# Program order on four engines at the output projections' boundaries of a two-block network, on one Trainium2 core

## The chip, the cores and the metric

The kernel runs on one core of one Trainium2 chip. The metric is the device time of a whole execution in microseconds (us). Its engines each work through a queue of their own: PE (TensorE) multiplies, ACT (ScalarE) and DVE (VectorE) work on elements, POOL (GpSimd) does small work and issues a part of the DMAs, SP (SyncE) issues most DMAs. Semaphores alone tie the queues together, so an instruction that waits holds whatever stands behind it on its own engine.

## The reference

Two blocks over x of 512 tokens by 1024 features, batch 1, all in fp32. The first block mixes by two kinds of attention, attends to a memory of 256 tokens and ends with a swiglu layer. The second block has two layers with a condition c and positions: an mLSTM mixer and a latent attention (MLA), each followed by a squared-relu layer. What matters here is the frame around each part:

```python
mix = jnp.concatenate([o_f, o_c], axis=-1) @ w_out[l]
x = x + rms_norm(mix, g_mix_post[l])
h = rms_norm(x, g_mem_pre[l])
...
x = x + g1[:, None, :] * rmsnorm(y, norm_g[l, 1])
h = modulate(rmsnorm(x, norm_g[l, 2]), sh2, sc2)
```

The shifts, scales and gates of the second block come from `cond @ ada_w[l] + ada_b[l]`, a vector times a matrix of 1024 by 6144 in each layer, and a smaller matrix `kv_ada_w`.

## The kernel before, in words

The tokens are four row tiles of 128, t = 0 to 3. x lies in SBUF as `x[t]`; before a product its normed rows are transposed, so that features lie on the partitions. Each fp32 product is three matmuls of a hi and a lo part (`prod`, lines 447 to 449). A weight block of 512 KB comes by DMA into one of four `raw` buffers (L423, SP's queue) and is split there: ACT writes the hi part (L307, or L317 with a gain), DVE subtracts it and writes the lo part (L308, L318). A block gives up its `raw` buffer when its last split is placed, which is when the next load can start. `pump` does this counting, `BUF["raw"]` is its limit, and `self.before` lists loads of x that go out ahead of a numbered weight block.

**A boundary** is where the output of one stage becomes the input of the next (`boundary`, L637). For each row tile t, `y_of(t)` multiplies (24 matmuls of 128x512 for the second half of an output projection), the squares of the result are summed on ACT (L579, `junk`), POOL makes a reciprocal root of it (`rstd`: L568, L562), DVE scales and adds it to x (L651, two halves), ACT squares the new x (L579), POOL makes the second `rstd`, and ACT writes the normed rows (L598, two halves). Then `put(t)`: eight transposes on PE (L609), in two stages of the network four scaled and shifted blocks on DVE (L616) and four on ACT (L619), then the hi part on ACT (L629, two) and the lo part on DVE (L630, two). With `fixed`, put(0) stands in the middle of product t = 2 and put(1) in the middle of product t = 3. The generator `first` is the head of the next stage: four accumulators of 24 matmuls of 128x256 for the tokens of row tiles 0 and 1 (tok0), then four for tiles 2 and 3 (tok1). So PE restarts with put(1)'s parts, and can hold out until tok1 needs put(2) and put(3).

`out_lin` (L716) calls `boundary` four times, with `fixed`: after `w_out`, after `w_mem_o`, after `a_w_out` and after `b_w_out`. I call these the first to the fourth boundary. Only the third and fourth scale and shift. `mlp` (L1344) calls it as well: after the swiglu (fixed), after the first squared-relu layer (not fixed), and for the last rows, where nothing follows.

**The order of the work** on each engine is not the order of the code. A scheduler plays the program through a simulated timeline and gives each engine its list. Work inside `hot` (`self.hot("hb")`) is lifted by a priority offset of 300. `ordered` (L692), which nothing called before, keeps the order of the code on PE, ACT, DVE and POOL for what it encloses.

Beside the main work, background steps compute the condition's rows (`row_by`, L859): pieces of `ada_w` come by POOL's DMAs (L878) into `araw`, DVE multiplies and adds them up (L873), folds the sum and splits it (L630), and then one matmul against a matrix of ones on PE (L891, the ones product) adds up over the partitions. Each `yield` ends a step; a step is taken for every 1.9 us of PE's work, and none inside a boundary.

The functions that the change touches, and those that call them:

Of the kernel before, what the change touches and what calls it, by code (L numbers as in the profile page):

```python
# [30 lines left out]
D_FF = 2816  # L31
ALL = slice(0, S)

BUF = dict(s8=14, u2=15, row=2, raw=4, w0=4, w1=4, w2=4, w3=5, w4=5, w5=5, w6=5, w7=5, ps=8, pace=1.9, pacb=1.9, man=0, lag=3, lagx=3, lagm=3, half=1, quiet=1, xp=0, fp=2, r1=1.25, r1b=3.6, r1c=2.4, r2=1.6, r2b=2.6, rx=1.4, rm=0.6, pre=10, gl=3, pl=0, hb=300, hs=0, ha=0, sp=0, spq=1.3, sq=1, b1=1, b2=1, lc=6, ar=4, mb=(6, 8, 6, 6, 6), mc=(4, 3, 4, 4, 4), st2=1, pr2=8, z1=4.5, z2=5, gt=3, rv=2, gs=1, rl=3, n1=4, ex=2, em=3, vg=1, sb=(8, 8, 6), mo=4, x1=2, g0=20, st=1, y1=0, y2=1, y3=0, ph=0, pq=0, fy=1, u1=6, s32=4, sm=60)

TWO_PI = 2.0 * np.pi

# [101 lines left out]
class Net:  # L139
    def __init__(self, tc, args, out, dbg=None, specs=None, pools=None):  # L140
        self.dry = specs is None
        self.specs = [] if self.dry else specs
        self.tc, self.a, self.out, self.dbg = tc, args, out, dbg or {}
        self.nc = Nothing() if self.dry else tc.nc
        self.cp, self.sb, self.ps, self.dr = pools
        self.uid = 0
        self.bg = None
        self.pace = 0.0
        self.quiet = self.late = False
        self.have = set()  # L150
        self.n_lo = self.n_load = self.n_take = 0
        self.n_ready = 0, 0
        self.raw_live = self.w_live = 0
        self.wcap = 0
        self.raws, self.ready = {}, {}
        self.pieces, self.credit = [], 0.0
        self.started, self.n_heads = None, 0
        self.gcols, self.before = {}, {}
# [45 lines left out]
    def pump(self):  # L204
# [4 lines left out]
        while more:  # L209
            more = False  # L210
            if self.n_load < len(self.specs):
                i = self.n_load
                kk, cc, loaders = self.specs[i][:3]
                if self.raw_live + len(loaders) <= BUF["raw"]:
                    self.raws[i] = [self.t("raw", [P, kk, cc], F32, BUF["raw"]) for _ in loaders]
                    for f in self.before.pop(i, ()):
                        f()
                    for loader, raw in zip(loaders, self.raws[i]):
                        loader(self, raw)
                    self.n_load += 1  # L220
                    self.raw_live += len(loaders)
                    more = True
            i, p = self.n_ready
            if i < self.n_load and self.w_live < self.wcap:
                kk, cc, loaders, gain = self.specs[i]
# [411 lines left out]
    def boundary(self, y_of, nxt, first, late=(1, 1, 2), fixed=True):  # L637
# [18 lines left out]
        def scaled(t):  # L656
            pend[t] = nxt(t, rs[t])

        hot = lambda: self.hot("hb")
        with nullcontext():  # L660
            for t in range(NT):
                g, n = y_of(t), 0
                while True:
# [407 lines left out]
    def mixer1(self):  # L1071
# [3 lines left out]
        get = lambda t: nc.sync.dma_start(out=self.x[t], in_=a["x"][0, tt(t), :])  # L1075
# [8 lines left out]
            nc.sync.dma_start(out=ext[:, 64:256], in_=rb)  # L1084
            nc.sync.dma_start(out=far, in_=rb[:, 191:192].rearrange("h o -> (h o)").partition_broadcast(P))

        self.before = {1: [lambda: get(1)], 3: [lambda: get(2), lambda: get(3)], 6: [biases]}
        h = HT(self, KD)
        vf = self.big([P, NT, S])
        with self.in_order():  # L1090
            self.mixer1_values(h, vf, w)
        self.cap(0)

        wg = self.weights(w, 0, KD, 1536, 8, gain="mix")
# [45 lines left out]
        vs, os, st = [vf, None], [None, None], {}  # L1140
# [37 lines left out]
        f, gs = fill(), self.gains()  # L1178
# [162 lines left out]
        return ho  # L1341


    def mlp(self, blocks, up, w_down, g, nxt, first, ready=None, caps=None, fixed=True):  # L1344

        nc, V = self.nc, self.nc.vector
        acc = [[self.u2() for _ in range(2)] for _ in range(NT)]
# [1 line left out]
        for b, nb in enumerate(blocks):  # L1349
# [26 lines left out]
            if last:  # L1376
# [6 lines left out]
                        ms += part(t, c, (yield from product(t, wgs[c])))  # L1383
                    return acc[t], ms

                self.boundary(y_of, nxt, first, fixed=fixed)
            else:
                for c in range(2):
                    wg = self.weights(w_down, k0, nb, c * S, S)
# [59 lines left out]
    def relu2(self, h, l, g, nxt, first, ready=None):  # L1449
# [23 lines left out]
                quarters.extend(self.quarters(h))  # L1473

        quarters = []
        self.mlp(BUF['mb'], up, self.a["mlp_w2_2"][l], g, nxt, first, ready, BUF['mc'], fixed=nxt is None)


    VW = 129
# [507 lines left out]
```

## Time and profile before

| | us |
|---|---|
| three runs, median | 1999.02 (1995.79 to 1999.51) |
| the profiled execution | 1995.13 |
| its span | 1993.3 |
| PE busy | 1941.7 (97% of the span) |
| DVE, ACT, POOL busy | 1276.1, 1037.3, 351.5 (64, 52, 18%) |
| granted TensorE clock, mean over the span | 0.991 |

The profiled execution lies 3.9 us under the median of the three runs. The page gives busy time by engine, the chain of work that ended last, and the waits; in the chain PE holds 90%, ACT and DVE 4% each. A row of a timeline has the start and length of an instruction (or of several alike, xN), its engine, line and tiles, and in brackets how long the engine had been idle before and what released it. Consecutive matmuls overlap in it: their starts, not their lengths, give the pace.

### The profile page before, as it was taken

To read this page: it belongs to the slowest core of one execution; us is meant where nothing else is said; L and a number is where in the kernel's file an instruction comes from. 1 tells how busy PE (TensorE), PEld (TensorE's weight loads), DVE (VectorE), ACT (ScalarE), POOL (GpSimd) and SP (SyncE) were. 2 spreads that over 40 slices of the span, in tenths; PEclk is the share of its full clock that TensorE was granted. 3 is DMA by queue.
4 is the path that set the end of the run, shared out by engine and by line. 5 is a ranking of instruction groups with operands and counts; after the bars stand their busy time and mean duration, and the time that the engine had idled before them with its cause. 6 is when DMAs were issued, how large, how long until landed. Compare 5 with 4: busy or idle time off the path is not lost.

```text
span 1993.3 us, 28466 instructions
## 1 busy us (share of the span) xinstructions
PE 1941.7 (97%) x10222; PEld 1645.7 (83%) x10222; DVE 1276.1 (64%) x2517; ACT 1037.3 (52%) x2282; POOL 351.5 (18%) x703
## 2 busy tenths in 40 slices
PE   7999999998999999999998999999999999999998
PEld 5888987878888888878877888888888879989987
DVE  5756655765766785666885557654458655656765
ACT  6767775456334343455646442433566555545443
POOL 1331111211221231212232222210020012000000
PEclk9999999999999999999999999999999999999999
DMA  6332333442655563345462446533042121233222
GB/s 202 91 80 65 117 125 112 145 138 64 190 181 164 175 212 127 103 128 154 125 192 94 126 161 222 165 112 119 29 126 69 64 85 43 75 107 116 96 82 77
DMA packets 175246, 241.95 MB, mean 121 GB/s; under 512 B 20107, under 2 KB 117536, under 8 KB 175104
## 3 DMA queue, kind: packets, MB, share of 16 engines
q1 hardware_dynamic: 150704, 170.53, 27.1%
q0 software_dynamic: 24400, 69.60, 11.4%
q8 instruction: 80, 1.31, 0.3%
q14 instruction: 62, 0.51, 0.1%
HBM read 237.88 MB, written 2.20 MB: 120 GB/s over the span
## 4 chain that ended last, share of the span: by engine, by line
PE 90%; ACT 4%; DVE 4%; issue 1%; DMA 0%; POOL 0%; SPq 0%; DVEq 0%; POOLq 0%; ACTq 0%
PE ps L447 25%; PE ps L448 24%; PE ps L449 24%; PE ps L510 6%; PE ps L1033 1%; PE ps L609 1%; PE ps L1823 1%; ACT s L317 1%; PE ps L1852 1%; PE ps L1004 1%; PE ps L1583 1%; DVE s L318 1%; PE ps L1017 1%; PE ps L1320 1%; ACT junk L579 1%
## 5 line engine op out<-in xcount | busy, mean ns | idle before, releaser
L447 PE MATMUL ps<-s,s 128*128 128x512 f32 (+3 forms) x2468 | 940.2, 383 | 28.5 <-ACT s L629 28.5
L448 PE MATMUL ps<-s,s 128*128 128x512 f32 (+3 forms) x2468 | 928.3, 377 | 0.1
L449 PE MATMUL ps<-s,s 128*128 128x512 f32 (+3 forms) x2468 | 924.4, 377 | 2.0 <-DVE s L630 2.0
L447 PEld LDWEIGHTS ps<-s,s 128*128 128x128 f32 (+1 forms) x2468 | 467.2, 190 | 114.6 <-ACT s L629 31.5
L449 PEld LDWEIGHTS ps<-s,s 128*128 128x128 f32 (+1 forms) x2468 | 466.3, 189 | 91.3 <-DVE s L630 2.5
L448 PEld LDWEIGHTS ps<-s,s 128*128 128x128 f32 (+1 forms) x2468 | 467.3, 189 | 83.7 <-DVE s L630 1.0
L307 ACT ACTIVATE s<-raw 128x512 fp32r<-128x512 f32 x329 | 186.3, 623 | 177.3 <-PE ps L449 130.7
L308 DVE TENSOR_TENSOR s<-raw,s 128x512 fp32r<-128x512 f32 x329 | 213.9, 688 | 87.8 <-ACT s L307 85.9
L873 DVE SCALAR_TENSOR_TENSOR u<-araw,cond,u 128x512 f32<-128x512 f32 x224 | 168.5, 752 | 31.9 <-DMA araw<-in_ada_w 21.9
L317 ACT ACTIVATE s<-raw,cols_all 128x256 fp32r<-128x256 f32 (+1 forms) x305 | 142.7, 544 | 59.5 <-PE ps L449 25.2
L318 DVE SCALAR_TENSOR_TENSOR s<-raw,cols_all,s 128x256 fp32r<-128x256 f32 (+1 forms) x305 | 146.2, 538 | 30.8 <-ACT s L317 30.5
L878 POOL DMA_DIRECT2D araw<-in_ada_w x192 | 104.2, 543 | 283.2 <-DVE u L873 236.2
L630 DVE TENSOR_TENSOR s<-u,s 128x512 fp32r<-128x512 f32 x118 | 80.1, 689 | 115.1 <-ACT s L629 92.6
L510 PEld LDWEIGHTS ps<-s,s 128*128 128x128 f32 x1092 | 130.2, 188 | 1.0
L568 POOL TENSOR_SCALAR sm<-sm,sm 128x1 f32<-128x1 f32 x34 | 16.5, 485 | 647.8 <-ACT junk L579 519.8
L510 PE MATMUL ps<-s,s 128*128 128x256 f32 x1092 | 130.5, 280 | 0.0
L629 ACT ACTIVATE s<-u 128x512 fp32r<-128x512 f32 x118 | 72.2, 627 | 53.6 <-PE ps L449 27.0
L630 DVE TENSOR_TENSOR s<-ps,s 128x512 fp32r<-128x512 f32 (+3 forms) x100 | 59.5, 606 | 36.9 <-ACT s L629 35.8
L1465 ACT ACTIVATE u<-ps 128x512 f32<-128x512 f32 x38 | 22.6, 596 | 114.9 <-PE ps L449 111.0
L1368 DVE TENSOR_TENSOR u<-ps,u 128x512 f32<-128x512 f32 x80 | 54.3, 687 | 39.7 <-PE ps L449 39.6
L629 ACT ACTIVATE s<-ps 128x512 fp32r<-128x512 f32 (+3 forms) x100 | 51.2, 526 | 23.5 <-PE ps L609 10.2
L318 DVE SCALAR_TENSOR_TENSOR s<-raw,cols_mix,s 128x128 fp32r<-128x128 f32 (+2 forms) x152 | 52.4, 401 | 11.0 <-ACT s L317 10.6
(261 smaller groups left out, 2011.0 us busy)
## 6 DMA issues: line engine op xcount, KB each, us to landing
raw<-in_mlp_w SPq DMA_DIRECT2D x128, 512.0 KB, 3.8
araw<-in_ada_w POOLq DMA_DIRECT2D x192, 256.0 KB, 3.4
raw<-in_w_gate_up SPq DMA_DIRECT2D x44, 512.0 KB, 4.5
raw<-in_w_in SPq DMA_DIRECT2D x24, 512.0 KB, 4.1
raw<-in_a_w_in SPq DMA_DIRECT2D x24, 512.0 KB, 4.6
raw<-in_w_down SPq DMA_DIRECT2D x22, 512.0 KB, 3.8
raw<-in_w_mem_kv SPq DMA_DIRECT2D x16, 512.0 KB, 3.5
araw<-in_kv_ada_w POOLq DMA_DIRECT2D x32, 256.0 KB, 3.6
```

What stands on the lines that cost most here:

```text
L307: A.activation(hi[:, sl, cl], src[:, sl, cl], AF.Copy)
L308: f.tensor_tensor(out=lo[:, sl, cl], in0=src[:, sl, cl], in1=hi[:, sl, cl].bitcast(F32), op=ALU.subtract)
L317: A.activation(hi[:, i, :], src[:, i, :], AF.Copy, scale=g)
L318: V.scalar_tensor_tensor(out=lo[:, i, :], in0=src[:, i, :], scalar=g, in1=hi[:, i, :].bitcast(F32), op0=ALU.mult, op1=ALU.subtract)
L447: self.nc.tensor.matmul(ps, lhsT=ah, rhs=bh, start=first and i == 0, stop=False)
L448: self.nc.tensor.matmul(ps, lhsT=ah, rhs=bl, start=False, stop=False)
L449: self.nc.tensor.matmul(ps, lhsT=al, rhs=bh, start=False, stop=last and i == n - 1)
L510: nc.tensor.matmul(ps, lhsT=l[:, k, :], rhs=m[:, k, :], start=first and k == e == 0, stop=k == 3 and e == 2, skip_group_check=True)
L629: self.nc.scalar.activation(hi, x, AF.Copy)
L630: self.nc.vector.tensor_tensor(out=lo, in0=x, in1=hi.bitcast(F32), op=ALU.subtract)
L873: V.scalar_tensor_tensor(out=acc, in0=raws.pop(j), scalar=vec[:, j:j + 1], in1=acc, op0=ALU.mult, op1=ALU.add)
L878: nc.gpsimd.dma_start(out=raws[j], in_=ws[:, j, :])
```

## The change

Three edits. (1) `out_lin`'s boundaries run inside `ordered`, so that on PE, ACT, DVE and POOL the order of the code holds, and nothing in them is lifted by `hot`; `mlp` now calls `boundary` with `fixed=False` throughout, which changes the swiglu's boundary alone: its transposes become `hot` and follow the products. (2) In the first stage three `raw` buffers may be in use rather than four, and the loads of x move: x[1] ahead of weight block 2 rather than 1, x[2] and x[3] ahead of block 4 rather than 3. SP's queue then begins x[0], gains, raw 0, raw 1, x[1], raw 2, raw 3, x[2], x[3]; before it began x[0], gains, raw 0, x[1], raw 1, raw 2, x[2], x[3], raw 3. (3) In the table `BUF`, y2 goes from 1 to 2: one more `yield` before the ones product of a background row.

```diff
@@ class Net, __init__ @@
         self.raw_live = self.w_live = 0
+        self.rcap = BUF["raw"] - 1
@@ pump @@
-                if self.raw_live + len(loaders) <= BUF["raw"]:
+                if self.raw_live + len(loaders) <= self.rcap:
@@ boundary @@
-        hot = lambda: self.hot("hb")
-        with nullcontext():
+        hot = nullcontext if fixed else lambda: self.hot("hb")
+        with self.ordered() if fixed else nullcontext():
@@ mixer1 @@
-        self.before = {1: [lambda: get(1)], 3: [lambda: get(2), lambda: get(3)], 6: [biases]}
+        self.before = {2: [lambda: get(1)], 4: [lambda: get(2), lambda: get(3)], 6: [biases]}
         h = HT(self, KD)
         vf = self.big([P, NT, S])
         with self.in_order():
             self.mixer1_values(h, vf, w)
+        self.rcap = BUF["raw"]
@@ mlp @@
-    def mlp(self, blocks, up, w_down, g, nxt, first, ready=None, caps=None, fixed=True):
+    def mlp(self, blocks, up, w_down, g, nxt, first, ready=None, caps=None):
...
-                self.boundary(y_of, nxt, first, fixed=fixed)
+                self.boundary(y_of, nxt, first, fixed=False)
@@ relu2 @@
-        self.mlp(BUF['mb'], up, self.a["mlp_w2_2"][l], g, nxt, first, ready, BUF['mc'], fixed=nxt is None)
+        self.mlp(BUF['mb'], up, self.a["mlp_w2_2"][l], g, nxt, first, ready, BUF['mc'])
```

How this moves instructions. In the rows below the line numbers of the changed kernel are one or two higher for the same code (L609 becomes L610, L629 L630, L891 L892), and tiles are named by what they are with a number: `ps` a PSUM bank, `s` a hi or lo part, `u` an SBUF row tile, `x_10` and `x_11` the row tiles t = 2 and 3.

First place: the first boundary, PE at the end of product t = 3. Before, put(1)'s transposes stood behind the product's last matmul, ahead of the next stage's first (128x256):

```order
1317 L449 MATMUL ps_3719<-s_768_3518,s_695_3173 128x512
1318 L447 MATMUL ps_3719<-s_768_3518,s_694_3172 128x512
1319 L448 MATMUL ps_3719<-s_768_3518,s_694_3172 128x512
1320 L449 MATMUL ps_3719<-s_768_3518,s_695_3173 128x512
1321 L609 MATMUL ps_3738<-ident_66,u_809_3702 128x128 x4
1322 L609 MATMUL ps_3743<-ident_66,u_810_3704 128x128 x4
1323 L447 MATMUL ps_3794<-s_802_3677,s_770_3531 128x256
1324 L447 MATMUL ps_3795<-s_802_3677,s_770_3531 128x256
1325 L448 MATMUL ps_3794<-s_803_3678,s_770_3531 128x256
1326 L449 MATMUL ps_3794<-s_802_3677,s_770_3531 128x256
```

Now they stand in the middle of the product, with twelve matmuls behind them:

```order
1307 L449 MATMUL ps_3721<-s_751_3401,s_692_3168 128x512
1308 L450 MATMUL ps_3721<-s_751_3401,s_693_3169 128x512
1309 L610 MATMUL ps_3740<-ident_66,u_809_3704 128x128 x4
1310 L610 MATMUL ps_3745<-ident_66,u_810_3706 128x128 x4
1311 L448 MATMUL ps_3721<-s_766_3505,s_694_3172 128x512
1312 L449 MATMUL ps_3721<-s_766_3505,s_694_3172 128x512
1313 L450 MATMUL ps_3721<-s_766_3505,s_695_3173 128x512
1314 L448 MATMUL ps_3721<-s_766_3505,s_694_3172 128x512
1315 L449 MATMUL ps_3721<-s_766_3505,s_694_3172 128x512
```

The same place on ACT. Before, the sixteen hi splits of four weight blocks stood ahead of put(1)'s parts (L629, last two rows):

```order
321 L579 ACTIVATE junk_3713,sm_3712<-x_10_91 128x1024
322 L317 ACTIVATE s_818_3726<-raw_3510,cols_all_1926 128x256 x4
323 L317 ACTIVATE s_819_3735<-raw_3523,cols_all_1926 128x256 x4
324 L317 ACTIVATE s_822_3758<-raw_3540,cols_all_1926 128x256 x4
325 L317 ACTIVATE s_823_3767<-raw_3557,cols_all_1926 128x256 x4
326 L579 ACTIVATE junk_3773,sm_3772<-ps_3719 128x512
327 L629 ACTIVATE s_802_3677<-ps_3738 128x4x128
328 L629 ACTIVATE s_804_3681<-ps_3743 128x4x128
```

Now two splits stand ahead of these parts (L630), and the rest of the splits behind them:

```order
318 L580 ACTIVATE junk_3715,sm_3714<-x_10_91 128x1024
319 L318 ACTIVATE s_818_3728<-raw_3510,cols_all_1926 128x256 x2
320 L630 ACTIVATE s_802_3679<-ps_3740 128x4x128
321 L630 ACTIVATE s_804_3683<-ps_3745 128x4x128
322 L318 ACTIVATE s_818_3728<-raw_3510,cols_all_1926 128x256 x2
323 L580 ACTIVATE junk_3775,sm_3774<-ps_3721 128x512
324 L599 ACTIVATE u_828_3779<-x_10_91,sm_3719 128x512
325 L599 ACTIVATE u_829_3781<-x_10_91,sm_3719 128x512
326 L580 ACTIVATE junk_3790,sm_3789<-x_11_92 128x1024
```

Second place: DVE some microseconds later, where it writes the lo parts of put(2). The casts and scalings between them (L774 ff.) belong to the tables of positions, whose numbers a DMA of POOL brings. Before, the first lo part of put(2) stood ahead of the first cast (337):

```order
333 L630 TENSOR_TENSOR s_805_3682<-ps_3743,s_804_3681 128x4x128
334 L318 SCALAR_TENSOR_TENSOR s_849_3992<-raw_3770,cols_all_1926,s_849_3992 128x256 x4
335 L318 SCALAR_TENSOR_TENSOR s_850_4009<-raw_3830,cols_all_1926,s_850_4009 128x256 x4
336 L630 TENSOR_TENSOR s_803_3678<-ps_3870,s_802_3677 128x4x128
337 L774 CAST sm_4096<-sm_4094 128x4
338 L630 TENSOR_TENSOR s_805_3682<-ps_3875,s_804_3681 128x4x128
339 L781 TENSOR_SCALAR u_861_4131<-u_860_4098,sm_4096 128x32 x4
340 L784 TENSOR_SCALAR araw_4136<-u_861_4131 128x128
341 L630 TENSOR_TENSOR s_803_3678<-ps_3918,s_802_3677 128x4x128
342 L786 CAST u_863_4138<-araw_4136 128x128
```

Now the cast (333) stands ahead of both, with splits and the tables' first steps between it and the first lo part (340):

```order
329 L652 SCALAR_TENSOR_TENSOR x_11_92<-u_776_3562,sm_3785,x_11_92 128x512
330 L652 SCALAR_TENSOR_TENSOR x_11_92<-u_827_3777,sm_3785,x_11_92 128x512
331 L319 SCALAR_TENSOR_TENSOR s_819_3737<-raw_3523,cols_all_1926,s_819_3737 128x256 x4
332 L319 SCALAR_TENSOR_TENSOR s_822_3760<-raw_3540,cols_all_1926,s_822_3760 128x256 x2
333 L775 CAST sm_4099<-sm_4097 128x4
334 L319 SCALAR_TENSOR_TENSOR s_822_3760<-raw_3540,cols_all_1926,s_822_3760 128x256
335 L782 TENSOR_SCALAR u_861_4134<-u_860_4101,sm_4099 128x32 x3
336 L319 SCALAR_TENSOR_TENSOR s_822_3760<-raw_3540,cols_all_1926,s_822_3760 128x256
337 L782 TENSOR_SCALAR u_861_4134<-u_860_4101,sm_4099 128x32
338 L785 TENSOR_SCALAR araw_4139<-u_861_4134 128x128
339 L787 CAST u_863_4141<-araw_4139 128x128
340 L631 TENSOR_TENSOR s_803_3680<-ps_3872,s_802_3679 128x4x128
```

Third place: PE behind the swiglu's boundary, where a ones product stands among the next stage's products. Before:

```order
3816 L447 MATMUL ps_8715<-s_1629_8583,s_1571_8253 128x512
3817 L448 MATMUL ps_8715<-s_1629_8583,s_1571_8253 128x512
3818 L449 MATMUL ps_8715<-s_1629_8583,s_1572_8254 128x512
3819 L891 MATMUL ps_8734<-u_1654_8711,onesr_78 128x512
3820 L447 MATMUL ps_8747<-s_1599_8388,s_1569_8249 128x512
3821 L448 MATMUL ps_8747<-s_1599_8388,s_1569_8249 128x512
```

Now the ones product of the row ahead of it in the list (128x320) comes in this stretch, 47 rows further on, and the one of before comes a hundred rows later:

```order
3863 L448 MATMUL ps_8738<-s_1613_8545,s_1562_8252 128x512
3864 L449 MATMUL ps_8738<-s_1613_8545,s_1562_8252 128x512
3865 L450 MATMUL ps_8738<-s_1613_8545,s_1563_8253 128x512
3866 L892 MATMUL ps_8768<-u_1645_8722,onesr_78 128x320
3867 L946 MATMUL ps_8799<-ident_66,u_1629_8621 128x8 x4
3868 L946 MATMUL ps_8806<-ident_66,u_1633_8629 128x8 x4
```

## Rows read from the trace of the kernel before

**Rows 1.** Page, part 1: busy us (share of the span), instructions.
```profile
PE 1941.7 (97%) x10222; PEld 1645.7 (83%) x10222; DVE 1276.1 (64%) x2517; ACT 1037.3 (52%) x2282; POOL 351.5 (18%) x703
```

**Rows 2.** Waits of PE: us in total, times, longest.
```profile
PE ps L447 <- ACT s L629: 28.5, 9, 6.1
```

**Rows 3.** Timeline of PE at the first boundary: start us, us, instruction, [idle before <-releaser].
```profile
334.21 1.04 PE L609 MATMUL ps<-ident,u 128*128 128x128 f32 x8
...
340.11 0.80 PE L447 MATMUL ps<-s,s 128*128 128x256 f32 x2 [4.86 <-ACT s L629]
...
345.59 0.28 PE L448 MATMUL ps<-s,s 128*128 128x256 f32 x1
...
347.00 0.29 PE L448 MATMUL ps<-s,s 128*128 128x256 f32 x1
```

**Rows 4.** Timeline of PE at the other three boundaries.
```profile
471.41 0.79 PE L447 MATMUL ps<-s,s 128*128 128x256 f32 x2 [5.03 <-ACT s L629]
...
475.35 0.28 PE L447 MATMUL ps<-s,s 128*128 128x256 f32 x1
...
1082.16 0.79 PE L447 MATMUL ps<-s,s 128*128 128x256 f32 x2 [6.13 <-ACT s L629]
...
1086.32 0.28 PE L447 MATMUL ps<-s,s 128*128 128x256 f32 x1
...
1640.65 0.80 PE L447 MATMUL ps<-s,s 128*128 128x256 f32 x2 [4.85 <-ACT s L629]
...
1646.84 0.28 PE L449 MATMUL ps<-s,s 128*128 128x256 f32 x1
```

**Rows 5.** Timeline of ACT at the first boundary.
```profile
332.53 6.48 ACT L317 ACTIVATE s<-raw,cols_all 128x256 fp32r<-128x256 f32 x16
...
339.48 1.06 ACT L629 ACTIVATE s<-ps 128x512 fp32r<-128x512 f32 x2
```

**Rows 6.** Timelines of POOL and DVE behind the first boundary.
```profile
346.90 0.84 POOL L201 DMA_DIRECT2D sm<-in_positions  x1
...
351.08 0.17 DVE L774 CAST sm<-sm 128x4 f32<-128x4 int32 x1 [1.55 <-DMA sm<-in_positions]
```

**Rows 7.** Timeline of ACT at the second and third boundaries.
```profile
464.22 6.08 ACT L317 ACTIVATE s<-raw,cols_all 128x256 fp32r<-128x256 f32 x15
...
1074.15 4.26 ACT L307 ACTIVATE s<-raw 128x512 fp32r<-128x512 f32 x8
...
1078.88 1.48 ACT L619 ACTIVATE u<-ps,cols,cols 128x128 f32<-128x128 f32 x4
...
1081.47 0.63 ACT L629 ACTIVATE s<-u 128x512 fp32r<-128x512 f32 x1
```

**Rows 8.** Windows: granted clock (PEclk) at a restart and around the L891 wait.
```profile
340.00:346.00 6.00, 5.84 (x27) 5.55 (x28) 5.98 (x13) 6.00 (x14) 0.56 (x1) 0.54 0.78 260
...
880.00:900.00 20.00, 17.23 (x75) 13.71 (x74) 15.01 (x21) 7.97 (x11) 4.74 (x9) 1.00 0.28 81
```

**Rows 9.** Timelines of PE and DVE at the ones product that waits.
```profile
892.62 0.47 PE L891 MATMUL ps<-u,onesr 128*128 128x512 f32 x1 [2.77 <-DVE u L630]
...
891.79 0.69 DVE L630 TENSOR_TENSOR u<-u,u 64x512 fp32r<-64x512 f32 x1
```

**Rows 10.** Timelines of PE and ACT in the first stage.
```profile
28.65 0.79 PE L447 MATMUL ps<-s,s 128*128 128x512 f32 x1 [3.30 <-ACT s L629]
...
29.66 1.91 PE L609 MATMUL ps<-ident,u 128*128 128x128 f32 x8
...
24.05 0.60 ACT L1061 ACTIVATE s<-ps 128x512 f32<-128x512 f32 x1 [2.24 <-PE ps L449]
...
29.26 5.09 ACT L317 ACTIVATE s<-raw,cols_mix 128x128 fp32r<-128x128 f32 x17
```

**Rows 11.** Timelines of POOL and DVE at the third boundary.
```profile
1079.08 2.43 POOL L568 TENSOR_SCALAR sm<-sm,sm 128x1 f32<-128x1 f32 x1 [4.40 <-ACT junk L579]
...
1077.05 4.29 DVE L308 TENSOR_TENSOR s<-raw,s 128x512 fp32r<-128x512 f32 x7
```

More of the change, by code (lines that the diff above doesn't have):

```diff
@@ L32 @@
 ALL = slice(0, S)
-BUF = dict(s8=14, u2=15, row=2, raw=4, w0=4, w1=4, w2=4, w3=5, w4=5, w5=5, w6=5, w7=5, ps=8, pace=1.9, pacb=1.9, man=0, lag=3, lagx=3, lagm=3, half=1, quiet=1, xp=0, fp=2, r1=1.25, r1b=3.6, r1c=2.4, r2=1.6, r2b=2.6, rx=1.4, rm=0.6, pre=10, gl=3, pl=0, hb=300, hs=0, ha=0, sp=0, spq=1.3, sq=1, b1=1, b2=1, lc=6, ar=4, mb=(6, 8, 6, 6, 6), mc=(4, 3, 4, 4, 4), st2=1, pr2=8, z1=4.5, z2=5, gt=3, rv=2, gs=1, rl=3, n1=4, ex=2, em=3, vg=1, sb=(8, 8, 6), mo=4, x1=2, g0=20, st=1, y1=0, y2=1, y3=0, ph=0, pq=0, fy=1, u1=6, s32=4, sm=60)
+BUF = dict(s8=14, u2=15, row=2, raw=4, w0=4, w1=4, w2=4, w3=5, w4=5, w5=5, w6=5, w7=5, ps=8, pace=1.9, pacb=1.9, man=0, lag=3, lagx=3, lagm=3, half=1, quiet=1, xp=0, fp=2, r1=1.25, r1b=3.6, r1c=2.4, r2=1.6, r2b=2.6, rx=1.4, rm=0.6, pre=10, gl=3, pl=0, hb=300, hs=0, ha=0, sp=0, spq=1.3, sq=1, b1=1, b2=1, lc=6, ar=4, mb=(6, 8, 6, 6, 6), mc=(4, 3, 4, 4, 4), st2=1, pr2=8, z1=4.5, z2=5, gt=3, rv=2, gs=1, rl=3, n1=4, ex=2, em=3, vg=1, sb=(8, 8, 6), mo=4, x1=2, g0=20, st=1, y1=0, y2=2, y3=0, ph=0, pq=0, fy=1, u1=6, s32=4, sm=60)
 TWO_PI = 2.0 * np.pi
```

## The prediction

> **What bounds the kernel now.** I read the page first: PE is busy 97% of a span of 1993.3 us [rows 1], so only its idle 52 us, and matmuls that run slower than they can, are to be had. Next the waits of PE: 28.5 us, more than half of them, are PE waiting to begin a product for a hi part that ACT writes [rows 2]. Then PE's timeline, gap by gap: four of these nine waits stand at the four boundaries of the output projections, 4.86, 5.03, 6.13 and 4.85 us [rows 3, 4], together 20.87. Behind each, matmuls start about 0.21 apart until a certain row, and then 12 of them take 1.41 (345.59 to 347.00 [rows 3]), 0.1175 each. The granted clock in that stretch is 0.54 [rows 8], the lower level, 1.2 GHz. What this costs: 23 matmuls in 5.48 us at the first boundary, 2.8 more than at 0.1175; 16 in 3.94 at the second, 2.05 more; 12 and eight transposes (0.8 at full clock) in 4.16 at the third, 1.95 more; 22 and eight transposes in 6.19 at the fourth, 2.8 more. In all 9.6, and **30.4 us** with the waits.
>
> Last, ACT's timeline says why PE waits. At the first boundary ACT is free at 332.53, but spends 6.48 us there on sixteen weight splits before it comes to put(1)'s two hi parts at 339.48 [rows 5]; PE had been through since 335.25. The second boundary has fifteen splits, 6.08 us, in the same place, the third eight, 4.26 us [rows 7].
>
> **Edit 1, program order.** Nothing is computed more or less. The order of the code puts put(1)'s transposes twelve matmuls before the end of product t = 3, and its parts behind two splits. Per boundary:
>
> First. From ACT's 332.53: two splits, 2 x 6.48/16 = 0.8, and two hi parts, 1.06 [rows 5], give 334.4; a lo part of 0.7 (the line's length on DVE [rows 9]) 335.1. PE ends its product, transposes included, at 335.0. The wait and its slow matmuls go: 4.86 + 2.8. What is late next is the tok1 half. The cast of the positions now stands ahead of put(2)'s lo parts on DVE. POOL issued that DMA at 346.90 and DVE had it at 351.08 [rows 6], 4.2 us. POOL still issues it behind x_11's second rstd. From PE's 335.0: a junk of 0.6, POOL 0.9, the update of x 1.4, its square 1.1, POOL 0.9 give 339.9, so the cast comes at 344.1. Behind it on DVE stand two lo parts of put(2), about seven splits of 0.4, table steps and the lo parts of put(3), some 6.5 us, to 350.6; PE has 96 matmuls of 0.1175 and sixteen transposes (1.6), and is through at 347.9. So a new wait of 2.7, and the gain is 7.65 - 2.7 = **4.95**. Bounds of that wait: 0, if splits fall elsewhere, to 4.2, the DMA's whole time.
>
> Second. The same order without a cast; I leave one split (6.08/15 = 0.4 [rows 7]) in front: 5.03 + 2.05 - 0.4 = **6.7**. Bounds 0 to 2 left.
>
> Third. put(1) must also be scaled and shifted. ACT is free at 1074.15 [rows 7]: two splits of 0.53 (4.26/8), four blocks 1.48, two hi parts 1.2 (0.6 each, the row at 1081.47), a lo part 0.7, and it is 1078.6. PE ends its product at 1076.03 (1082.16 less 6.13 [rows 4]). That leaves 2.6; since DVE's blocks have to pass splits as well I take 2.9, and for put(3)'s transposes and tok1's parts 2.8 more, five or six splits' length. Gain 6.13 + 1.95 - 5.7 = **2.4**. This counts on the full clock after a gap of 2.9. A gap of 2.77 [rows 9] left it at 1.00 [rows 8]; one of 3.30 in the first stage was followed by eight transposes in 1.91 us [rows 10] against 1.04 [rows 3]. 2.9 is nearer to the former; with the latter the gain is 2 less.
>
> Fourth. The same chain as at the third, 2.75 at the restart, 1.5 behind: 4.85 + 2.8 - 4.25 = **3.4**, again 2 to 2.8 less with a lower clock.
>
> Together 17.4; the bounds are 30.4 and, with the larger waits, about 8.
>
> What this order may cost: POOL. At the third boundary an L568 of POOL took 2.43 us and ended at 1081.51, while DVE went through seven splits L308 from 1077.05 to 1081.34 [rows 11]; elsewhere the line takes about 0.25. It lay under PE's long wait. In the new order rstd is what put(2) and put(3) hang on, with splits beside it. My 2.8 and 1.5 above contain one such hold between them. The Trainium skill ("SBUF — State Buffer", section on the two separate sides) says that a DVE instruction with two SBUF inputs and a POOL instruction that reads SBUF exclude each other for the whole of an instruction, whichever begins first. The trace agrees in that POOL came through when the splits ended, but it stayed out for seven of them, not for one; by the page's one instruction (4.29/7 = 0.6 us) the two holds that I count would be 1.8 shorter each, and the forecast 3.6 lower, inside my range.
>
> The swiglu's boundary has no wait of PE on either side today that shows among the waits; its lifted transposes cost or give nothing that I can see: 0, with bounds of -0.5 and +2 (half a third boundary).
>
> **Edit 3, the ones product a step later.** Today one ones product holds PE for 2.77 us: its lo part is done only at 892.48, behind a chain of gate work on DVE [rows 9]. In the new order the product in this stretch belongs to the row before, 47 rows later on PE, about 9 us later, and that row's parts are computed by about 900, just before its turn. Gain **2.8**; bounds 0 to 2.8, and a new wait of up to 2 in a bad case. The remaining steps move some 60 us later in all; the rows are due later still.
>
> **Edit 2, the first stage.** PE's restart at 28.65 hangs on hi parts of put(2) on ACT. The new list has twelve more splits ahead of these parts, of 0.3 each (5.09/17 [rows 10]): 3.6 us, of which ACT's idle 2.24 before 24.05 and some 0.65 from an earlier start of the products (raw 1 is loaded before x[1]) take most. I take **+0.5**, bounds -1 to +4.
>
> **Sum.** -(4.95 + 6.7 + 2.4 + 3.4 + 2.8) + 0.5 = -19.75. On the profiled execution, 1995.1, that is 1975.4. The median of the runs shown lies 3.9 above it; how a later median falls between I can't tell, so I start halfway, at 1997.0, and forecast **1977**.
>
> **The rivals.**
> *A clean restart everywhere.* If neither the cast nor the modulated chain nor POOL leave a wait, all 30.4 and 2.8 go: 1997.0 - 33.2 = 1964. For it: the waits fall where PE has 48 to 96 matmuls in hand. Against: ACT's chain of 1078.6 against 1076.03.
> *The third and fourth keep their gaps.* If a modulated restart waits 3.3 or more, the clock drops as it did after 3.30, and POOL's 2.43 comes on top: both gain about nothing, or lose 1. Then 4.95 + 6.7 + 2.8 - 0.5, less 1 to 3 for the first stage's upper bound, some 12: 1985.
> *The change does not move the end.* The waits go from the restart to put(3)'s transposes and tok1 in full, and the ones product finds another chain: 1995 to 2003. Against it: at tok1 PE has 11 us of matmuls in hand that it did not have at the restart.
> *Slower, because strict order stops PE three times.* No engine may pass what waits. PE stands at the restart (2.9), at put(3)'s transposes while POOL is held by DVE's splits (2.43) and at tok1 behind DVE (2.7); 8.0 in all, with 2.8 for a lower clock 10.8. Today a boundary costs 30.4/4 = 7.6. If all four come to this, that is 3.2 x 4 = 12.8 worse, less 2.8, plus 0.5: 2007. It decides where the three waits and the slow matmuls pass 7.6 at one boundary. Against it: the first two have no modulated blocks, and no L568 near them as long as at the third.
>
> **How the numbers follow.** My forecast, 1971 to 1983, gets 0.55; the clean restart 0.15; the kept gaps 0.15; no effect 0.07; slower 0.08. Measurement tells about 0.2%, 4 us, from no change. Faster by that is 0.85, same 0.07, slower 0.08. The range takes in the clean case and the kept gaps with the first stage's upper bound, and leaves out the last two cases: 1963 to 1991.
>
> **What would show it.** In the waits, "L447 <- ACT L629" falls from 28.5 to under 15, and the longest to under 3.5. At the first boundary no gap at 335 and a new one near 348, with DVE's lo part as its releaser. At the second none over 1. At the third and fourth about 2.9 at the restart, with windows at full clock. The ones product's 2.8 is gone from the waits. The first stage's gap lies between 2 and 5. I am wrong if a restart of the first two boundaries still waits for ACT over 2 us, if new waits on POOL (transposes waiting for normed rows) pass 3 us, or if windows behind a boundary still show a clock under 0.9.

## The result and the profile after

The changed kernel takes **1981.79 us** (median of 6 runs, 1981.05 to 1985.93) against 1998.97 before (6 runs, 1995.79 to 1999.51). The ratio is 0.9922, 95% interval 0.9909 to 0.9935: 0.8% faster, 16 us by the ratio and 17 by the medians. The forecast was 1977, in a range from 1963 to 1991, with 0.85 on faster by more than 0.2%. Between the two profiled executions the difference is smaller, 1995.13 to 1981.73 or 13.4 us; the experiments say why in part.

The page's first part and the waits of PE, after (us in total, times, longest), to be held against [rows 1, 2]:

```profile
PE 1938.7 (98%) x10222; PEld 1641.1 (83%) x10222; DVE 1281.8 (65%) x2517; ACT 1036.4 (52%) x2282; POOL 349.9 (18%) x703
```
```profile
PE ps L448 <- ACT s L630: 16.4, 10, 4.1
...
PE ps L610 <- DVE u L1625: 3.1, 1, 3.1
...
PE ps L449 <- DVE s L631: 1.7, 4, 0.8
...
PE ps L892 <- DVE u L631: 0.4, 1, 0.4
```

The waits for ACT's hi parts fell from 28.5 to 16.4, as many times as before and one more. The ones product's 2.8 is 0.4. A wait that I had left alone, of transposes in the mLSTM stage for a tile that DVE writes (L1625), rose from 2.2 to 3.1. PE's timeline, after, with every wait that the next part speaks of:

```profile
29.44 0.80 PE L448 MATMUL ps<-s,s 128*128 128x512 f32 x1 [3.90 <-ACT s L630]
...
333.84 1.26 PE L610 MATMUL ps<-ident,u 128*128 128x128 f32 x8 [0.49 <-ACT u L599]
...
338.41 0.39 PE L448 MATMUL ps<-s,s 128*128 128x256 f32 x1 [0.52 <-ACT s L630]
...
353.42 0.39 PE L449 MATMUL ps<-s,s 128*128 128x256 f32 x1 [0.76 <-DVE s L631]
...
460.06 1.27 PE L610 MATMUL ps<-ident,u 128*128 128x128 f32 x8 [0.47 <-ACT u L599]
...
464.65 0.39 PE L448 MATMUL ps<-s,s 128*128 128x256 f32 x1 [0.53 <-ACT s L630]
...
892.81 0.38 PE L892 MATMUL ps<-u,onesr 128*128 128x320 f32 x1 [0.38 <-DVE u L631]
...
1029.24 0.66 PE L610 MATMUL ps<-ident,u 128*128 128x128 f32 x4 [3.09 <-DVE u L1625]
...
1062.29 1.27 PE L610 MATMUL ps<-ident,u 128*128 128x128 f32 x8 [0.56 <-ACT u L599]
...
1070.46 0.58 PE L448 MATMUL ps<-s,s 128*128 128x256 f32 x1 [4.11 <-ACT s L630]
...
1075.62 0.28 PE L448 MATMUL ps<-s,s 128*128 128x256 f32 x1
...
1086.46 0.62 PE L448 MATMUL ps<-s,s 128*128 128x256 f32 x2
...
1628.36 0.42 PE L448 MATMUL ps<-s,s 128*128 128x256 f32 x1 [3.08 <-ACT s L630]
...
1632.02 0.28 PE L450 MATMUL ps<-s,s 128*128 128x256 f32 x1
```

At the first and second boundaries the 4.86 and 5.03 of [rows 3, 4] are 0.5 for the transposes and 0.5 for the parts, and at the first another 0.76 at tok1. At the third, 4.11 are left of 6.13, at the fourth 3.08 of 4.85. The windows (PEclk is the third number from the end) show the clock behind the first boundary, behind the mLSTM wait, and behind the third and fourth boundaries:

```profile
338.00:344.00 6.00, 5.25 (x42) 5.05 (x43) 4.48 (x8) 4.62 (x11) 0.91 (x3) 1.00 0.42 150
...
1028.00:1034.00 6.00, 4.76 (x23) 3.97 (x24) 3.58 (x6) 1.75 (x3) 0.00 (x0) 1.00 0.39 118
1070.00:1076.00 6.00, 5.39 (x25) 5.10 (x26) 4.51 (x7) 4.47 (x9) 1.69 (x3) 0.53 0.39 146
1628.00:1634.00 6.00, 5.33 (x31) 5.10 (x32) 4.51 (x7) 4.47 (x9) 1.02 (x2) 0.72 0.40 126
```

The clock stays at 2.4 GHz (1.00) at the first boundary, where it had been 0.54 [rows 8]; at the third and fourth the lower level still comes, until 1075.62 and 1632.02.

How far each stage moved is read from rows that both traces have, as the time after less the time before. It is +1.8 behind the first stage, -3.0 behind the first boundary (matmuls of L1303 at 384.23 and 381.27), -11.0 behind the ones product (L945 at 904.12 and 893.12), -10.8 ahead of the third boundary (the mLSTM wait ends at 1040.00 and 1029.24) and -10.8 again at its tok1 (1097.30 and 1086.46), -10.45 ahead of the fourth (L1834 at 1602.36 and 1591.92) and -13.2 behind it (L510 at 1712.37 and 1699.20).

### The profile page after: what moved, and what is told of

It is laid out like the page before. It is cut to its first block, busy times and chain, and to the rows that moved or that the text cites. A ratio compares the mean times of both kernels' runs of the same rounds, so it can differ in the third digit from the quotient of the medians.

```text
span 1979.8 us, 28458 instructions
## 1 busy us (share of the span) xinstructions
PE 1938.7 (98%) x10222; PEld 1641.1 (83%) x10222; DVE 1281.8 (65%) x2517; ACT 1036.4 (52%) x2282; POOL 349.9 (18%) x703
## 5 line engine op out<-in xcount | busy, mean ns | idle before, releaser
L448 PE MATMUL ps<-s,s 128*128 128x512 f32 (+3 forms) x2468 | 938.9, 382 | 16.5 <-ACT s L630 16.4
L308 ACT ACTIVATE s<-raw 128x512 fp32r<-128x512 f32 x329 | 186.5, 622 | 193.5 <-PE ps L450 141.0
L309 DVE TENSOR_TENSOR s<-raw,s 128x512 fp32r<-128x512 f32 x329 | 221.0, 713 | 84.1 <-ACT s L308 82.7
L874 DVE SCALAR_TENSOR_TENSOR u<-araw,cond,u 128x512 f32<-128x512 f32 x224 | 167.6, 748 | 23.0 <-DMA araw<-in_ada_w 16.4
L569 POOL TENSOR_SCALAR sm<-sm,sm 128x1 f32<-128x1 f32 x34 | 13.9, 408 | 586.6 <-ACT junk L580 458.9
L630 ACT ACTIVATE s<-u 128x512 fp32r<-128x512 f32 x118 | 72.2, 628 | 50.1 <-DVE u L1432 24.6
L630 ACT ACTIVATE s<-ps 128x512 fp32r<-128x512 f32 (+3 forms) x100 | 50.8, 525 | 23.6 <-PE ps L610 6.8
```

The source lines that it names most:

```text
L308: A.activation(hi[:, sl, cl], src[:, sl, cl], AF.Copy)
L309: f.tensor_tensor(out=lo[:, sl, cl], in0=src[:, sl, cl], in1=hi[:, sl, cl].bitcast(F32), op=ALU.subtract)
L448: self.nc.tensor.matmul(ps, lhsT=ah, rhs=bh, start=first and i == 0, stop=False)
L630: self.nc.scalar.activation(hi, x, AF.Copy)
L874: V.scalar_tensor_tensor(out=acc, in0=raws.pop(j), scalar=vec[:, j:j + 1], in1=acc, op0=ALU.mult, op1=ALU.add)
```

## The experiments

All ratios are to the kernel before, timed on the same chip, with a 95% interval. The runs stand on several chips, and the changed kernel was timed in a batch of its own; the kernel before took 1998.97 to 1999.86 by its medians in the four batches, so that a difference of 1 us between two kernels of different batches says nothing. In what was expected, theory is what I held after reading the two traces.

**The three edits alone.** First the kernel before, unchanged, a second time:

> The kernel before once more, with a second profile. Its runs so far fall at 1995.8 and around 1999, and the profiled execution (1995.1) was of the low kind. Theory: the difference of some 3.5 us is the TensorE clock, granted low behind one of the waits of 2 to 3.3 us in some executions and not in others; a profile near 1999 then shows one more stretch at the lower clock (the 2.77 us wait at the ones product or the 2.16 at the mLSTM stage first), and the span grows by the same 2 to 4 us. Rival: the time lies outside the span or is spread evenly, and no single stretch shows it.

Measured 1999.88 (10 runs, 1995.14 to 2001.41), ratio 0.9999 [0.999, 1.0009]. The 35 executions of the kernel before in this batch tell the clock: those at a mean granted clock of 0.991 took 1995.1 to 1996.9, those at 0.988 to 0.990 took 1997.3 to 2001.9. Both profiles fell on an execution of the first kind, so the stretch itself was not seen for this kernel. That the slower executions have lower clocks is shown; where, is not. Most of the latter lie 3 us or more behind the former, and one fall of the clock at the mLSTM wait costs some 1.7 (an estimate, in the last section), so that place alone would not explain them.

Edit 1 alone (the hunks `boundary`, `mlp` and `relu2` of the diff):

> The first edit alone (program order at the four boundaries, lifted transposes at the swiglu's). If the edits add up as the two traces suggest (the offset between them moves by -4.8 at the first boundary, about -6 at the second, 0 at the third, -2.7 at the fourth, +0.7 at the swiglu's and +0.9 at the mLSTM stage), it is 12 to 13 us faster than before: 1986, ratio 0.9938. Rival: the order needs the other two edits (first stage, background) to bring its gain; then 0.996 or above.

1988.81, ratio 0.9947 [0.9931, 0.9964], 10.6 us by the ratio. The waits at the four boundaries are those of the changed kernel (0.53, 0.53, 4.12, 3.10). What is short is at the ones product, which now waits longer than before the change, and behind it the clock falls. PE's timeline and a window of this run:

```profile
884.73 0.77 PE L891 MATMUL ps<-u,onesr 128*128 128x512 f32 x1 [3.22 <-DVE u L630]
```
```profile
884.00:888.00 4.00, 3.27 (x8) 2.63 (x9) 2.12 (x4) 0.72 (x2) 2.00 (x4) 0.51 0.04 6
888.00:892.00 4.00, 4.00 (x13) 3.14 (x12) 2.90 (x4) 0.00 (x0) 2.20 (x4) 0.64 0.60 176
```

Edit 2 alone (`rcap` and `self.before`):

> The second edit alone (three raw buffers and later loads of x in the first stage). Theory: it costs what the offset at 67 us shows in the changed kernel, +1.8: 2000.8, ratio 1.0009, with the wait ahead of the second half of the first product at 3.9 rather than 3.3. Rival, my forecast's upper end of a gain: the first products start 0.65 earlier and the time does not grow: 0.9995 to 1.0000.

2000.88, ratio 1.0009 [1.0, 1.0018]. The wait at the half of the first product is 3.89 as expected, but the rows behind the stage lie only 0.2 later than in the second profile of the kernel before (72.91 and 72.70). The +1.8 of the first pair of profiles is mostly not the edit: the same rows lie at 73.98 and 73.85 in the runs of edit 1 and edit 3, whose first stage is that of before.

This run has the stretch that I had looked for. The mLSTM wait is 2.16, as in the kernel before, and here the clock falls behind it, at 1040 to 1048, where the profile of before has 1.00 for the same wait:

```profile
1041.05 0.66 PE L610 MATMUL ps<-ident,u 128*128 128x128 f32 x4 [2.16 <-DVE u L1625]
```
```profile
1040.00:1044.00 4.00, 2.95 (x12) 2.51 (x13) 4.00 (x7) 1.31 (x3) 1.21 (x3) 0.77 0.85 280
1044.00:1048.00 4.00, 4.00 (x16) 3.19 (x15) 2.68 (x5) 0.34 (x1) 1.95 (x4) 0.80 0.90 307
```

Edit 3 alone (y2 = 2):

> The third edit alone (a row's ones product one background step later). Theory: the wait of 2.77 us at the ones product goes to under 0.5 and nothing else moves: -2.4, 1996.6, ratio 0.9988. Rival: with the old order the product of that stretch meets another chain, and the wait stays over 2: 1.0000.

1995.54, ratio 0.9980 [0.9971, 0.9990], 4.3 us by medians. The wait is 0.48. The profile gains nothing all the same (span 1993.9), because the mLSTM wait grew from 2.16 to 3.04 and there the clock fell, and because its first stage lies 1.1 later (the 73.85 above). The runs lie closer together (1994.6 to 1997.5) than those of before: with the 2.77 gone, fewer of them catch a low clock, which fits the first experiment but is not a proof of where.

**Without edit 2.** The changed kernel with `rcap` and `self.before` as they were:

> The changed kernel with its second edit undone (four raw buffers and the old loads of x; program order and the later ones product stay). Theory: the edits add up, and the second costs the 1.0 us that it cost alone: 1980.8, ratio to before 0.9907. Rival: with the earlier start of the first products it is worth something in the changed kernel, and this one is slower than 1982, 0.993.

1981.67, ratio 0.9913 [0.9899, 0.9927]; the changed kernel has 1981.79. Edit 2 is worth nothing that can be told here. With edit 1 alone at 1988.81, edit 3 on top of it is worth some 7 us, not 2.8: it takes away the 3.22 and the clock's fall behind it.

**Why the third boundary gained nothing.** Timelines of ACT and DVE in the changed kernel from product t = 3 on:

```profile
1063.12 1.42 DVE L652 SCALAR_TENSOR_TENSOR x<-u,sm,x 128x512 f32<-128x512 f32 x2 [0.24 <-POOL sm L563]
...
1064.63 1.06 ACT L580 ACTIVATE junk<-x 128x1024 bf16<-128x1024 f32 x1 [1.78 <-DVE x L652]
...
1065.69 1.14 ACT L308 ACTIVATE s<-raw 128x512 fp32r<-128x512 f32 x2
...
1066.34 1.29 DVE L309 TENSOR_TENSOR s<-raw,s 128x512 fp32r<-128x512 f32 x2 [1.80 <-ACT s L308]
1067.55 1.36 DVE L617 TENSOR_SCALAR u<-ps,cols,cols 128x128 f32<-128x128 f32 x4
...
1068.39 1.50 ACT L620 ACTIVATE u<-ps,cols,cols 128x128 f32<-128x128 f32 x4 [1.56 <-DVE u L617]
1069.77 1.16 ACT L630 ACTIVATE s<-u 128x512 fp32r<-128x512 f32 x2
...
1071.85 0.60 ACT L580 ACTIVATE junk<-ps 128x512 bf16<-128x512 f32 x1
...
1084.38 1.50 ACT L620 ACTIVATE u<-ps,cols,cols 128x128 f32<-128x128 f32 x4 [1.54 <-DVE u L617]
1085.76 1.16 ACT L630 ACTIVATE s<-u 128x512 fp32r<-128x512 f32 x2
```

It reads as a chain over two engines. DVE ends the update of x_10 at 1064.5; ACT squares it until 1065.7, and only then splits (L308). DVE's lo splits follow these, DVE's scaled blocks (L617) follow the lo splits, and ACT's blocks wait 1.56 for DVE's, because they write the same tile (in the last kernel below each engine writes a half of its own, and ACT's blocks begin without such a wait). So put(1)'s hi part begins at 1069.77, while PE was through at 1066.35. Behind it ACT comes to the square sum of product t = 3 at 1071.85 only, 5.5 after PE had it ready, and from there the normed rows of put(3) are late too.

The first repair keeps splits out of products t = 2 and t = 3 until the transposes are placed:

```diff
 def tick(self, cost):
+    if self.hold:
+        return
...
+                self.hold = bool(nxt) and t >= 2 and fixed
...
                     if n == 4 and nxt and t >= 2 and fixed:
                         self.put(*pend.pop(t - 2))
+                        self.hold = False
```

> The changed kernel, but no weight split is placed between the start of products t = 2 and t = 3 and the transposes in their middle, so that ACT and DVE come to put(1)'s blocks and parts before the two splits. Theory: at the third and fourth boundary PE waits 4.11 and 3.08 because DVE's scaled blocks stand behind two splits, which stand behind ACT's square of x_10; without them the blocks begin at the end of the update of x_10, some 3 us earlier, the restarts wait 1 to 2 us and the clock stays up: about -8, 1974, ratio 0.9873. Rival: the blocks wait for the update of x_10 anyway (POOL's reciprocal root and DVE's two halves stand ahead of them), the waits shrink by one split's length (0.6) and the clock still falls: 1980, 0.991. Second rival: the two splits are late for the next stage's products, a wait for a weight part takes the place: no gain, 0.992.

1981.09, ratio 0.9907 [0.9893, 0.9920]. The restarts went as the theory had it, 1.39 at the third and under 0.4 at the fourth. PE's timeline, at tok1 of the first and third boundaries:

```profile
353.82 0.38 PE L452 MATMUL ps<-s,s 128*128 128x256 f32 x1 [2.08 <-DVE s L634]
...
1087.64 0.62 PE L451 MATMUL ps<-s,s 128*128 128x256 f32 x2 [1.67 <-ACT s L633]
```

The first was 0.76 in the changed kernel, the second nothing. By rows that both traces have, this profile is 1.9 later than the changed kernel's behind the first boundary, where splits are now late; 0.7 of it has come back by the ones product. Another 1.5 go at the mLSTM wait, where the clock fell in this execution (0.75 in a window of 1028 to 1034) and not in that of the changed kernel; this is not the repair's doing. The third boundary adds nothing, and the fourth takes 4.2 off. Both of the last edits together:

> Both of these together: the second edit undone, and parts before splits. Theory: they add up, -9 against the changed kernel, about 1973, 0.987. Rival: as of the two alone.

1978.84, ratio 0.9898 [0.9885, 0.9912]: some 2 us below the one before, at the edge of what these runs tell apart.

The second repair holds splits only in product t = 3 of the two modulated boundaries (`n_out` counts the calls of `out_lin`, `held` the cost that `tick` passed over), and places the ones held right behind put(1):

```diff
+                self.hold, self.held = bool(nxt) and t == 3 and fixed and self.n_out >= 3, 0.0
...
                         self.put(*pend.pop(t - 2))
+                        self.hold = False
+                        while self.held >= BUF["spq"] and self.pieces:
+                            self.held -= BUF["spq"]
+                            self.piece()
```

> The changed kernel, with splits held back only in product t = 3 of the third and fourth boundaries, and made up for right behind put(1). Theory: the restarts wait 1.4 and 0.4 as in the run that held them everywhere (4.11 and 3.08 in the changed kernel), while its two new waits, 2.08 at the first boundary's tok1 and 1.67 at the third's, do not come, since no split falls behind there: at least -5, 1976.5, and 1974 if the clock stays up as well. Rival: the made-up splits only stand in front of the next link (the square sum of product t = 3, the normed rows of put(2)), and the wait moves to tok1 or put(2): 1980 to 1982.

**1977.70** (1976.94 to 1978.93), ratio 0.9895 [0.9881, 0.9908], below both kernels. PE's timeline and two windows:

```profile
1067.72 0.38 PE L453 MATMUL ps<-s,s 128*128 128x256 f32 x1 [1.40 <-ACT s L635]
...
1084.88 0.62 PE L453 MATMUL ps<-s,s 128*128 128x256 f32 x2 [1.66 <-ACT s L635]
...
1625.70 0.38 PE L453 MATMUL ps<-s,s 128*128 128x256 f32 x1 [0.37 <-ACT s L635]
```
```profile
1084.00:1090.00 6.00, 5.12 (x21) 4.51 (x22) 3.77 (x7) 3.42 (x7) 0.00 (x0) 0.72 0.22 59
1626.00:1632.00 6.00, 5.66 (x48) 5.58 (x47) 5.39 (x9) 4.31 (x10) 1.19 (x2) 1.00 0.42 142
```

The fourth boundary is clean. At the third the restart is 2.7 earlier and tok1 1.6 (1084.88 against 1086.46), and 1.66 of waiting have moved there: the rival held for a half. What was won at tok1 is lost again behind it, where the clock falls (the 0.72). ACT takes the first result of tok1 at the same time in the changed kernel and in this one:

```profile
1092.93 0.60 ACT L1467 ACTIVATE u<-ps 128x512 f32<-128x512 f32 x1 [3.93 <-PE ps L450]
```
```profile
1092.91 0.60 ACT L1478 ACTIVATE u<-ps 128x512 f32<-128x512 f32 x1 [5.50 <-PE ps L455]
```

So the third boundary as a whole gains nothing here either, and all of the 4.2 between the two spans (1979.8 and 1975.6) comes at the fourth.

Then PE's wait filled with work, so that the clock alone changes:

```diff
+            if t == NT - 1 and self.n_out >= 3 and not self.dry:
+                d = self.bank()
+                for _ in range(44):
+                    self.nc.tensor.matmul(d[:, 0:P], lhsT=self.onesr, rhs=self.onesr, start=True, stop=True)
```

> The changed kernel with 44 matmuls of 128x128 on a matrix of ones, whose result nobody reads, behind product t = 3 of the third and fourth boundaries (some 2.6 us of PE in waits of 4.11 and 3.08). Theory: the restart comes at the same moment, but the clock stays at 2.4 GHz: 21 and 14 slow matmuls go, -2 and -1.4, together with what falls out of step behind them -3.4 to -4: 1978. Rival: the clock falls with what PE waits for over a longer stretch than this gap, or the filler delays the restart: no change, 1982, or slower.

1982.90, ratio 0.9919 [0.9906, 0.9933], no gain. The clock did stay up: the mean is 0.997 in this run and 0.994 in the changed kernel. But the 44 took 4.9 us, not 2.6, from 1067.81 to 1072.67 at the third boundary. At the fourth they end at 1631.56, and ACT had the hi part by 1629.9 (its row of two begins at 1629.27), so there the filler spoils most of what the clock gave. The third is clearer: there ACT begins the two parts at 1071.40, so the first is done at about 1072.0 and the filler costs 0.7. PE at its tok1, and a window behind its restart:

```profile
1088.07 0.61 PE L449 MATMUL ps<-s,s 128*128 128x256 f32 x2 [2.02 <-ACT s L631]
```
```profile
1072.00:1078.00 6.00, 6.00 (x53) 5.98 (x53) 4.51 (x7) 4.46 (x11) 1.70 (x3) 1.00 0.42 124
```

From the end of product t = 3 to tok1's first matmul it is 21.3 us before (1076.03 to 1097.30), 20.1 in the changed kernel (1066.35 to 1086.46), 20.1 with the filler (1067.97 to 1088.07) and 18.6 with the second repair (1066.32 to 1084.88). With 21 slow matmuls or with none, tok1 comes as late, and ACT begins put(3)'s two hi parts 1.6 later with the filler (1087.37 and 1085.76), as much as the product ends later: put(3)'s chain on ACT and DVE sets it, and the restart and its clock lie under that chain. The 1.6 by which this run is late at the third boundary are lost just ahead of it, at the mLSTM wait (3.41 here, and a clock of 0.72 from 1029 to 1035). From there on the filler costs nothing at the third boundary and gains 0.4 to the end.

**Three more.** The swiglu's boundary as before:

```diff
-        hot = nullcontext if fixed else lambda: self.hot("hb")
-        with self.ordered() if fixed else nullcontext():
+        hot = nullcontext if fixed and strict else lambda: self.hot("hb")
+        with self.ordered() if fixed and strict else nullcontext():
...
-                self.boundary(y_of, nxt, first, fixed=False)
+                self.boundary(y_of, nxt, first, fixed=fixed, strict=False)
```

> The changed kernel with the swiglu's boundary as before (transposes in the middle of the products, not lifted; the four output projections keep program order). Theory: the 0.73 us wait that PE has at 851 us goes and with it at most 1 us: 1981, 0.9913. Rival: the lifted transposes had a gain of their own that the wait hides, and this one is slower than the changed kernel by 1 us or more: 0.993.

1984.09 (1981.30 to 1985.29), ratio 0.9919 [0.9906, 0.9933]. The wait of 0.73 is gone, and nothing came of it; the spread is that of the changed kernel. Inconclusive within 2 us.

Program order at the first two boundaries only:

```diff
+        strict = fixed and self.n_out < 3
-        hot = nullcontext if fixed else lambda: self.hot("hb")
+        hot = nullcontext if strict else lambda: self.hot("hb")
-        with self.ordered() if fixed else nullcontext():
+        with self.ordered() if strict else nullcontext():
```

> The changed kernel, but program order only at the first and second boundaries; the third and fourth are scheduled as before. Theory: the order brought nothing at the third (the offset to the kernel before is -10.7 ahead of it and -10.5 behind) and 2.7 at the fourth: 1984.5, ratio 0.9927. Rival, by my forecast's own terms (2.4 and 3.4): 1987.6, 0.9943.

1983.83, ratio 0.9924 [0.9912, 0.9937], 2.0 above the changed kernel. The waits are 6.15 and 4.87 again. By the ratios the two are not told apart (0.9924 and 0.9922); by rows that both traces have, this run lies 0.3 ahead of the changed kernel behind the third boundary and 2.1 behind it at the end. So program order is worth nothing at the third and somewhat over 2 us at the fourth, and the forecast had 5.8 for the two.

Last, several known waits at once, on the second repair:

```diff
         def biases():
+            nc.sync.dma_start(out=self.posi, in_=a["positions_2"].rearrange("o (t p) -> p (o t)", p=P))
...
-                    if j < 2:
+                    if i == 1:
                         self.nc.vector.tensor_scalar(out=y[:, j, :], in0=ps[:, j, :], scalar1=gj, scalar2=sj,
```

> The last kernel with three more things: the second edit undone; the positions loaded in the first stage on SP's queue, so that the cast at the first boundary has nothing to wait for; and of put's scaled blocks DVE takes one row half and ACT the other (two blocks of each half before), so that ACT does not wait for DVE within a half. Theory: -0.8 to -2.7 for the cast (0.76 us waited in the changed kernel, 2.08 where splits were held), -1 for the first stage, -0.7 at each modulated put that PE waits for: 1972 to 1974. Rival: these waits are covered by matmuls in hand and only the first stage's counts: 1 us below the kernel before this one.

1980.84, ratio 0.9909 [0.9894, 0.9924], slower than the second repair. PE does what was expected: its waits at tok1 of the first and third boundaries are gone, the time from product to tok1 at the third is 16.8, and its last matmul starts at 1965.03, against 1967.85 with the second repair. The loss comes after the last result. Rows of the output's transfers (issue of the first and the last), of the second repair and of this kernel:

```profile
L659 SPq DMA_DIRECT2D out<-x x8: 332/333/363, 1952.5 to 1972.3; - x8
```
```profile
L658 SPq DMA_DIRECT2D out<-x x8: 332/332/363, 1949.7 to 1969.5; - x8
...
DMA to landing us min/median/max: 2.0/2.0/2.1
```

The spans are 1975.6 and 1979.3. The last transfer lands some 2 us after its issue in both; then 1.2 us pass in the one and 7.8 in the other. What holds the end is POOL's closing instruction, a DRAIN. Its rows (shortest, median and longest in ns, first and last start) in the second repair and in this kernel:

```profile
L1996 POOLq DRAIN  x3: 46/98/1344, 1970.2 to 1975.3; - x3
```
```profile
L1996 POOLq DRAIN  x3: 46/93/11146, 1967.4 to 1979.1; - x3
```

The first of the three takes 1.34 us there and 11.15 here, until 1978.56, and the other engines' last instructions follow it. Why it takes so long here stays open.

## Why the prediction was right, and where it was off

The mechanism was right at the first two boundaries and in part at the fourth: ACT's splits ahead of put(1)'s parts were what the change took out of PE's way, and at the first two the lower clock went with the waits (1.00 in the window of 338 to 344 and, at the second, from 464 to 470). Three of the forecast's own signs came out against it: the waits for ACT's hi parts are 16.4 (under 15 was said), the longest is 4.1 (under 3.5), and behind the third and fourth boundaries windows show a clock under 0.9, which it had named as a sign of being wrong. By the prediction's own steps:

- First boundary, -4.95: -4.8. The term came out by two errors against each other. The cast cost 0.76 at tok1 and not 2.7, and put(1)'s transposes and parts waited 1.0 that I had at nothing. These two would leave some 5.9; where the rest went is not traced.
- Second, -6.7: -6.1 by its waits and slow matmuls (7.1 before, 1.0 after).
- Third, -2.4: nothing. **This step failed.** "ACT is free at 1074.15: two splits, four blocks, two hi parts" counted ACT's queue alone. The blocks are on two engines, ACT's wait for DVE's, and DVE's stood behind two lo splits that waited for ACT. The first repair moved these splits and the restart came down to 1.4. And I added the restart and tok1 as if each were paid: the filler shows that tok1's chain decides when tok1 begins, whatever the restart does. The remark that a restart of 3.3 or more would lose the clock was the rival's, and it is what the profile shows (4.11, clock 0.53).
- Fourth, -3.4: -2.7. Restart 3.08 for 2.75, and the clock fell (0.72).
- POOL: the hold of 2.43 [rows 11] did not come back as a term. In the changed kernel L569 takes at most 0.72 at the third boundary, and no run of seven splits stands beside it on DVE. The prediction speaks of one such hold in its 2.8 and 1.5 and then of two; two of 2.43 would not fit into these 4.3. The lateness was there, but it was that of ACT and DVE. No run here shows a step where the Trainium skill's rule ("SBUF — State Buffer", two separate sides) decided.
- Edit 3, -2.8: **undersized**. -2.4 in the profiles, but -4.3 alone and about -7 beside program order, by medians. The wait's price was read from a profile in which the clock stayed at 1.00 behind 2.77; in the run of edit 1 it fell to 0.51 behind 3.22.
- Edit 2, +0.5: 1.0 alone by the medians and 1.8 by the ratio (interval 0 to 3.6), 0.1 in company. Right in size, as far as these runs tell.
- The swiglu's boundary (0) cost 0.7, and the mLSTM wait, which I did not look at, 0.9. The latter goes with edit 3: the wait is 3.04 with edit 3 alone, and 2.16 with edit 1 or edit 2 alone.

The sum, -19.75, against -17 by medians and -13.4 by the profiles. That these two differ is the step "how a later median falls between I can't tell": the profiled execution of before was of its quicker kind, and the changed kernel's was like its median. The kept gaps, which I gave 0.15 and 1985, describe the third boundary, and the clock at the fourth, better than my forecast does; the total lies between the two. That it fell well inside the range owes something to terms that missed in opposite directions, the third boundary and edit 3.

## What to carry to other kernels

A strict order is worth most where one engine's late work stood alone in the way; where the chain goes back and forth between two engines, follow it on both, and look at what comes last in the stage before adding up what comes first. An idle stretch in front of the matrix engine is not a gain until the next thing that it waits for has moved as well. A price taken from one profile can hide a lower clock that most executions pay (30 of the 35 of the kernel before lie below 0.991): list the granted clock of every run beside its time.

## What was not expected of the hardware

The clock behind a wait of 2 to 3 us is not the same in every run. Behind 2.16 us at the same place it stayed at 1.00 in the profiles of the kernel before and fell to 0.77 and 0.80 in the run of edit 2; behind 3.09 it stayed at 1.00 in the changed kernel, and behind 3.10 in the first repair, in the same place, a window of 1028 to 1034 has 0.75. Of the fourteen profiled executions seven show the fall at this place: one of the four with a wait of 2.16, five of the nine with 3.04 to 3.11, and the one with 3.41. Each fall costs about 1.7 us, by an estimate (four times 0.23 and 0.20 in the run of edit 2). A difference of this size between two profiles is not to be put down to an edit before this place has been looked at. The changed kernel's own runs split that way: 1981.05 to 1981.85 at a mean clock of 0.994, 1984.95 at 0.993 and 1985.93 at 0.992. And a matmul of 128x128 on this data type is not cheaper than one of 128x256 at the same clock: 44 took 4.86 us, 0.11 each, against 0.1175. What sets this pace was not separated: in a window of 1067.8 to 1072.7 of that run the clock is 1.00, and the weight loads (PEld), one for each matmul, are busy for 4.89 of 4.90 us.
